# Rows 16 to 31 of the triangular matrices held in a PSUM bank for the substitution steps of a hybrid decoder trunk

## The chip, the cores and the metric

The kernel runs on one core of a Trainium2 chip. The metric is the device time of one execution in microseconds (us); lower is better. TensorE (PE in the profile) does the matrix products, VectorE (DVE), ScalarE (ACT) and GpSimd (POOL) the elementwise work, and SyncE (SP) issues the DMAs. Each engine works through a queue of instructions of its own.

## What is computed

Two layers of a decoder trunk on 512 tokens of width 1024. One input projection feeds three groups of heads side by side (RWKV-7 time mixing, causal pooling, native sparse attention); one output projection, a gated ConvFFN and a gated per-layer embedding follow. The change lies in the RWKV-7 mixer, whose recurrence over the tokens is

```
def step(S, inp):
    r_t, w_t, k_t, v_t, kk_t, a_t = inp
    sa = jnp.einsum('bhvk,bhk->bhv', S, -kk_t)
    S = (S * w_t[:, :, None, :] + sa[..., None] * (kk_t * a_t)[:, :, None, :]
         + v_t[..., None] * k_t[:, :, None, :])
    return S, jnp.einsum('bhvk,bhk->bhv', S, r_t)
...
_, y = lax.scan(step, S0, xs)
```

The kernel does it in chunks of 64 tokens. Within a chunk every token's `sa` depends on those of the tokens ahead of it in the chunk, which is a triangular system: for each of 8 chunks and 4 heads a 64x64 unit triangular matrix is inverted, 32 matrices in all for a layer.

## The kernel before

Everything is float32. A product that must be exact is split into a rounded part and its rest (`whi`, `wlo` for the weights, `xhl` for the activations) and done as three matmuls: L159, L160 and L161 in the helper `gemm`, 512 columns each. ACT makes `whi` (L132); `wlo` (L133) is made by POOL or by DVE, whichever a call of `wsplit` names.

The triangular matrices are inverted in 32x32 diagonal blocks. `IN` (tile `inn`, 128 partitions x 32 x 32) holds the blocks; the partitions are the 64 blocks (32 matrices, two blocks each), twice: DVE writes partitions 0 to 63 with a transpose (L415), ACT copies them to 64 to 127 (L417). The upper copy lets the lower half of the partitions work on even columns of the inverse and the upper half on odd ones. `QI` is the inverse, which POOL sets to the identity first (L421 to L423; `after(...)` makes the first of these wait for L417). Then the generator `rwkv()` runs 31 substitution steps on DVE, t = 1 to 31. Each is a multiply of the columns so far with row t of `IN`, broadcast over the columns (L434, m x (t+1) elements for each partition with m = (t+1)//2, into `prd`), and a sum of the products (L436, back into `QI`). After step 31 a copy (L438) and three transposes (L441 twice, L443) put the blocks where TensorE reads them. TensorE makes the off-diagonal blocks in two rounds of 32 small matmuls (L450 from `Q11`, shown as `q` in the trace, and then L458), and the recurrence over the eight chunks, `chain`, follows: per chunk the products g (L502, L506), u (L513), s (L521) and y (L536, L539).

Beside the substitution runs the projection work of the attention: `tokmaj` and `tokval` turn operands of the recurrence into token order on TensorE (L474 `bkt`, L485 `vt`), the projection onto tokens (L637 to L639, `tok`), the compression of keys and values (L654, `cmp`), and `roped` for four query tiles, then for two key tiles: a projection `z` of 24 matmuls, a shuffle of it (L588, DVE, from PSUM), a product with the cosines (L589, DVE, one operand in PSUM), two POOL instructions (L590, L591), a rounding on ACT (L599 or L596), the rest on DVE (L600 or L597), and DMAs into `qs` or `ku`. The compressed scores `sct` (L693) and their transposes `scp` (L707) stand on TensorE just ahead of L450. After L450 and L458 TensorE does two more projections (tiles p0 and p1 of `z`) between the first g, u and s, then the attention scores (L755 onwards).

What stands where on an engine is chosen ahead of time by a scheduler from the order in which the code is written, from `pace`, which slips pieces of `rwkv()` between the matmuls of `gemm`, and from the scheduler's own estimate of durations. The code hands out eight PSUM banks by tag: `rw` has three. `bkt`, `vt`, the blocks of L450 and L458, and all of `chain` take their banks from `rw`.

Of the kernel before, what the change touches and what calls it, by code (L numbers as in the profile page):

```python
# [12 lines left out]
ALU = mybir.AluOpType  # L13
AX = mybir.AxisListType

P = 128
# [27 lines left out]
def hybrid(tc, xT, pT, pos, cst, msk, par, gfin, w_in, w_tok, w_out, w_up, w_down, w_pg, w_pp,  # L44
           lora, wcmp, pe, wpool, out):
    nc = tc.nc
    V, S, G, TE = nc.vector, nc.scalar, nc.gpsimd, nc.tensor
    from contextlib import ExitStack
    ctx = ExitStack()
    with ctx:  # L50
# [8 lines left out]
        def nm(s):  # L59
            cnt[0] += 1  # L60
            return f"{s}_{cnt[0]}"
# [3 lines left out]
        def unit(shape, name, dt=F32, tag="r"):  # L65
            return mp.tile(shape, dt, tag=tag, name=nm(name), bufs=NB[tag])

        def psum(name, tag="sc"):
            return pp.tile([P, 512], F32, tag=tag, name=nm(name), bufs={"mm": 2, "rw": 3, "sc": 2, "o": 1}[tag])
# [189 lines left out]
        for l in range(L):  # L259
# [130 lines left out]
            for u in range(4):  # L390
                if u == 2:
                    mixed(7, VM[:, 1, :])
                for h2 in range(2):
                    a = slice(h2 * 64, h2 * 64 + 64)
# [19 lines left out]
            IN = unit([P, 32, 32], "inn")  # L414
            V.transpose(IN[0:64].rearrange("p a b -> p (a b)"), ND.rearrange("p a b -> p (a b)"))  # L415
            V.memset(IN[0:64].rearrange("p a b -> p (a b)")[:, 0:1024:33], 1.0)
            ti = S.copy(IN[64:128], IN[0:64])  # L417
            QI = unit([P, 32, 32], "qi")
            PRD = unit([P, 16, 32], "prd", tag="n")
            qf = QI.rearrange("p a b -> p (a b)")  # L420
# [9 lines left out]
            def rwkv():  # L430
                for t in range(1, 32):
                    m = (t + 1) // 2
                    qv = QI[:, 0:2 * m:2, :]
                    V.tensor_tensor(PRD[:, 0:m, 0:t + 1], qv[:, :, 0:t + 1],  # L434
                                    IN[:, t, 0:t + 1].unsqueeze(1).to_broadcast([P, m, t + 1]), op=ALU.mult)
                    V.tensor_reduce(qv[:, :, t], PRD[:, 0:m, 0:t + 1], axis=AX.X, op=ALU.add)  # L436
                    yield 0.3 + m * (t + 1) * 2.1e-3
                V.tensor_copy(QI[0:64, 1:32:2, :], QI[64:128, 0:32:2, :])  # L438
                Q11 = unit([32, 32, 32], "q11")
                for b in range(2):  # L440
                    V.transpose(TT_[b * 32:(b + 1) * 32, :, b * 32:(b + 1) * 32].rearrange("p i s -> p s i"),  # L441
                                QI[b * 32:(b + 1) * 32].rearrange("p j s -> p s j"))
                V.transpose(Q11.rearrange("p i j -> p j i"), QI[0:32])  # L443
                yield 4.0
                ZS = unit([64, 32, 32], "zs")
                for u in range(2):
                    ps = psum("z12", "rw")
                    for i in range(16):
                        n = u * 16 + i
                        TE.matmul(ps[32:64, i * 32:(i + 1) * 32], XM[n // 8][0:32, (n // 4) % 2, n % 4, 32:64],  # L450
                                  Q11[:, n, :], start=True, stop=True)
                    S.copy(ZS[32:64, u * 16:(u + 1) * 16, :].rearrange("p a b -> p (a b)"), ps[32:64, :])
                yield 1.5
                for u in range(2):
                    ps = psum("t12", "rw")
                    for i in range(16):
                        n = u * 16 + i
                        TE.matmul(ps[0:32, i * 32:(i + 1) * 32], ZS[32:64, n, :], TT_[32:64, n, 32:64],  # L458
                                  start=True, stop=True)
                    S.copy(TT_[0:32, u * 16:(u + 1) * 16, 32:64], ps[0:32, :].rearrange("p (a b) -> p a b", b=32))  # L460
                yield 1.5
                yp = None
                for c in range(NCK):
                    yp = yield from chain(c, yp)
# [27 lines left out]
            def chain(c, yp):  # L492
# [77 lines left out]
                return yp  # L570

            pace.start(rwkv(), 3.0)
            pace.tick(0.1)
            tokmaj()
# [66 lines left out]
            for t in range(4):  # L641
# [5 lines left out]
                            op=ALU.mult)  # L647
# [27 lines left out]
            for j in range(4):  # L675
# [4 lines left out]
                for g in range(2):  # L680
                    a = slice(g * 64, g * 64 + 64)
                    b = slice(64 - g * 64, 128 - g * 64)
# [19 lines left out]
            for cp2 in range(2):  # L702
# [6 lines left out]
                for c2 in range(2):  # L709
# [3 lines left out]
                                    op=ALU.add)  # L713
# [13 lines left out]
            for ty in range(2):  # L727
# [3 lines left out]
                for g in range(2):  # L731
                    a = slice(g * 64, g * 64 + 64)
                    b = slice(64 - g * 64, 128 - g * 64)
# [65 lines left out]
            for cp2 in range(2):  # L799
# [8 lines left out]
                for j2 in range(2):  # L808
                    a = slice(j2 * 64, j2 * 64 + 64)
# [148 lines left out]
            for n in range(KD):  # L958
# [5 lines left out]
                for h in range(HV):  # L964
                    a = slice(h * T // HV, (h + 1) * T // HV)
# [24 lines left out]
        for h in range(2):  # L990
            a = slice(h * 256, h * 256 + 256)
# [174 lines left out]
```

## Time and profile before

| | |
|---|---|
| median of three runs | 1508.69 us (1508.46 to 1509.61) |
| the profiled execution | 1512.75 us, of which the span from the first to the last instruction is 1511.0 us |
| TensorE busy | 1456.0 us, 96% of the span |
| VectorE, ScalarE, GpSimd busy | 824.3, 677.1 and 738.6 us |
| mean granted TensorE clock | 0.980 of full speed |

The profile is of one execution. Its page gives the busy time of each engine; the timeline lists instructions in order with the idle time ahead of each and what ended it; the windows give busy time and granted clock of chosen stretches. A TensorE matmul's shown duration overlaps the next one's, so the pace is read from one start to the next. [...]

### The profile page before, as it was taken

The page shows a single profiled execution, that of the slowest core. Times are in us where ns is not written, and L with a number is a line of the kernel's source. Part 1 is how long each engine was busy: PE and PEld are TensorE (multiplying, and loading weights), DVE is VectorE, ACT ScalarE, POOL GpSimd, SP SyncE. Part 2 cuts the span into 40 slices and gives each one's busy share as a digit, 9 for nine tenths or more (in the row PEclk, how much of TensorE's full clock was granted, in tenths as well). Part 3 has the DMA queues.
Part 4 walks back from the last instruction along what each step waited for, and adds up shares of the span by engine and source line. Part 5 has one row for each costly group of instructions (what it writes and reads, how often), then busy time and mean ns, then how long its engine had stood idle before and what let it go on. Part 6 is the DMA issues. An engine that isn't in the chain of part 4 may idle for free.

```text
span 1511.0 us, 21122 instructions
## 1 busy us (share of the span) xinstructions
PE 1456.0 (96%) x7634; PEld 1161.9 (77%) x7634; DVE 824.3 (55%) x1354; ACT 677.1 (45%) x1296; POOL 738.6 (49%) x621
## 2 busy tenths in 40 slices
PE   6999899999999999999999989899999999999997
PEld 4787666588888888888877867666888888888886
DVE  7769687425773155522567696772277712554234
ACT  5552265544443245443544425564454423444433
POOL 3355443275455455566614553533645555555653
PEclk9999799999999999999999989999999999999998
DMA  5234400042233333333422243001422333333332
GB/s 174 67 98 116 107 3 2 19 144 86 97 98 100 103 97 95 97 99 103 150 90 75 82 118 84 2 15 56 126 91 94 98 96 103 96 100 93 97 100 95
DMA packets 78985, 134.62 MB, mean 89 GB/s; under 512 B 10145, under 2 KB 20897, under 8 KB 78881
## 3 DMA queue, kind: packets, MB, share of 16 engines
q1 hardware_dynamic: 77728, 132.22, 29.2%
q8 instruction: 60, 0.98, 0.3%
q10 hardware_dynamic: 1152, 1.05, 0.2%
q14 instruction: 45, 0.36, 0.1%
HBM read 120.59 MB, written 4.19 MB: 83 GB/s over the span
## 4 chain that ended last, share of the span: by engine, by line
PE 84%; DVE 12%; issue 2%; ACT 1%; POOL 0%; DMA 0%; SPq 0%; DVEq 0%; ACTq 0%
PE up L161 11%; PE up L159 11%; PE up L160 11%; PE dn L161 5%; PE dn L159 5%; PE dn L160 5%; PE o L864 2%; PE z L161 2%; PE z L159 2%; PE ptp L856 2%; PE z L160 2%; PE wo L159 2%; PE wo L160 2%; PE wo L161 2%; PE pg L160 2%; PE pg L159 2%
## 5 line engine op out<-in xcount | busy, mean ns | idle before, releaser
L133 POOL TENSOR_TENSOR wlo<-raw,whi 128x512 fp32r<-128x512 f32 (+3 forms) x392 | 507.8, 1299 | 476.7 <-ACT whi L132 463.7
L132 ACT CAST whi<-raw 128x512 fp32r<-128x512 f32 (+3 forms) x440 | 261.2, 596 | 433.7 <-PE up L160 114.4
L159 PE MATMUL up<-xhl,whi 128*128 128x512 f32 x704 | 274.1, 389 | 0.0
L161 PE MATMUL up<-xhl,wlo 128*128 128x512 f32 x704 | 273.7, 389 | 0.0
L160 PE MATMUL up<-xhl,whi 128*128 128x512 f32 x704 | 273.6, 389 | 0.0
L160 PEld LDWEIGHTS up<-xhl,whi 128*128 128x128 f32 x704 | 132.1, 188 | 27.5
L161 PEld LDWEIGHTS up<-xhl,wlo 128*128 128x128 f32 x704 | 132.1, 188 | 27.5
L159 PEld LDWEIGHTS up<-xhl,whi 128*128 128x128 f32 x704 | 132.1, 188 | 27.2
L159 PE MATMUL dn<-ghl,whi 128*128 128x512 f32 x352 | 136.9, 389 | 0.0
L160 PE MATMUL dn<-ghl,whi 128*128 128x512 f32 x352 | 136.9, 389 | 0.0
L161 PE MATMUL dn<-ghl,wlo 128*128 128x512 f32 x352 | 136.3, 389 | 0.0
L159 PE MATMUL z<-xhl,whi 128*128 128x512 f32 x288 | 117.8, 410 | 7.3 <-ACT whi L132 6.4
L929 DVE SCALAR_TENSOR_TENSOR cv<-cv,par 128x511 f32<-128x511 f32 x88 | 77.9, 885 | 82.2 <-ACT cv L928 82.2
L161 PE MATMUL z<-xhl,wlo 128*128 128x512 f32 x288 | 116.6, 405 | 4.6 <-DVE wlo L133 4.6
L160 PE MATMUL z<-xhl,whi 128*128 128x512 f32 x288 | 116.5, 405 | 4.0 <-DVE xhl L192 3.9
L944 DVE TENSOR_TENSOR x<-x,dn 128x512 f32<-128x512 f32 x32 | 22.0, 688 | 166.4 <-PE dn L161 166.4
L931 DVE SCALAR_TENSOR_TENSOR cv<-cv,par 128x510 f32<-128x510 f32 x88 | 100.3, 1142 | 2.9
L927 DVE TENSOR_TENSOR cv<-up,rb 128x512 f32<-128x512 f32 x88 | 60.0, 684 | 74.1 <-PE up L161 59.8
L771 ACT ACTIVATE pb<-sc,smax 128x128 f32<-128x128 f32 (+3 forms) x128 | 66.8, 531 | 46.5 <-DVE smax L768 26.0
L928 ACT ACTIVATE cv<-cv,par 128x512 f32<-128x512 f32 x88 | 71.6, 815 | 31.4 <-DVE cv L927 31.4
L160 PEld LDWEIGHTS dn<-ghl,whi 128*128 128x128 f32 x352 | 66.1, 188 | 13.8
L161 PEld LDWEIGHTS dn<-ghl,wlo 128*128 128x128 f32 x352 | 66.1, 188 | 13.7
(299 smaller groups left out, 2626.2 us busy)
## 6 DMA issues: line engine op xcount, KB each, us to landing
raw<-in_w_up_dram SPq DMA_DIRECT2D x176, 256.0 KB, 2.7
raw<-in_w_in_dram SPq DMA_DIRECT2D x72, 256.0 KB, 2.8
raw<-in_w_down_dram SPq DMA_DIRECT2D x64, 256.0 KB, 2.6
raw<-in_w_out_dram SPq DMA_DIRECT2D x32, 256.0 KB, 2.8
raw<-in_w_pg_dram SPq DMA_DIRECT2D x32, 256.0 KB, 2.7
raw<-in_w_down_dram SPq DMA_DIRECT2D x32, 192.0 KB, 2.3
x<-in_xT_dram SPq DMA_DIRECT2D x16, 256.0 KB, 3.8
qs<-hl SPq DMA_DIRECT2D x32, 128.0 KB, 2.3
```

Source lines behind the costliest of these rows:

```text
L132: S.copy(hi[:, :ncol], raw[:, :ncol])
L133: (lo_eng or G).tensor_tensor(lo[:, :ncol], raw[:, :ncol], hi[:, :ncol].bitcast(F32), op=ALU.subtract)
L159: TE.matmul(ps, wh, xh, start=i == 0, stop=False)
L160: TE.matmul(ps, wh, xl, start=False, stop=False)
L161: TE.matmul(ps, wl, xh, start=False, stop=i == n - 1)
L771: S.activation(pb[:, ty, 0:w], srcs[ty], AF.Exp, bias=smax[:, g, ty:ty + 1], accum_out=ssum[:, g, ty:ty + 1])
L856: TE.transpose(ps[:, (g * 2 + j2) * P:(g * 2 + j2 + 1) * P], pbs[j2][g][:, ty, kb * P:(kb + 1) * P], ident)
L864: TE.matmul(op_[g * 64:g * 64 + 64, 0:256], VT[:, kb, ty * 128 + g * 64:ty * 128 + g * 64 + 64], pts[ty][:, g, :], start=False, stop=kb == ...
L927: V.tensor_tensor(u_, ps, rb, op=ALU.mult)
L928: S.activation(c_, u_, AF.Identity, scale=pc(PC2 + n), bias=pc(PCB + n))
L929: V.scalar_tensor_tensor(c_[:, 1:T], u_[:, 0:T - 1], pc(PC1 + n), c_[:, 1:T], op0=ALU.mult, op1=ALU.add)
L931: V.scalar_tensor_tensor(c_[:, 2:T], u_[:, 0:T - 2], pc(PC0 + n), c_[:, 2:T], op0=ALU.mult, op1=ALU.add)
```

## The change

Only rows 0 to 15 of `IN`, columns 0 to 15, are copied by ACT into partitions 64 to 127 now. A new tile `INP` takes one of the three `rw` banks; ACT copies rows 16 to 31 of `IN` into both of its halves, from partitions 0 to 63 (two copies of 64 x 512). Steps t = 16 to 31 read row t from `INP`, steps 1 to 15 from `IN` as before. `INP` holds its bank until step 31 has read it. Arithmetic and its order within a step are unchanged. Lines from 422 on stand four lines lower in the new kernel.

```diff
-            ti = S.copy(IN[64:128], IN[0:64])
+            ti = S.copy(IN[64:128, 0:16, 0:16], IN[0:64, 0:16, 0:16])
+
+            INP = psum("inp", "rw").rearrange("p (a b) -> p a b", b=32)
+            for b in range(2):
+                S.copy(INP[b * 64:(b + 1) * 64], IN[0:64, 16:32, :])
...
                     V.tensor_tensor(PRD[:, 0:m, 0:t + 1], qv[:, :, 0:t + 1],
-                                    IN[:, t, 0:t + 1].unsqueeze(1).to_broadcast([P, m, t + 1]), op=ALU.mult)
+                                    (IN[:, t, 0:t + 1] if t < 16 else INP[:, t - 16, 0:t + 1]).unsqueeze(1).to_broadcast([P, m, t + 1]), op=ALU.mult)
```

The scheduler gives a new order from here on. On VectorE, around step 15 of the first layer, it was (`ct`, `kcm` and `vcin` are small steps of the compressed keys that wait for `cmp` of TensorE; `wlo` is a weight's rest; `zt` and `qr` are the shuffle and the product of the first query tile):

```order
L133 TENSOR_TENSOR wlo_1293<-raw_1290,whi_1292 128x512
L434 TENSOR_TENSOR prd_681<-qi_680,inn_676 128x8x17
L436 TENSOR_REDUCE qi_680<-prd_681 128x8
L434 TENSOR_TENSOR prd_681<-qi_680,inn_676 128x9x18
L436 TENSOR_REDUCE qi_680<-prd_681 128x9
L588 STREAM_SHUFFLE zt_1269<-z_1146 128x512
L434 TENSOR_TENSOR prd_681<-qi_680,inn_676 128x9x19
```

and is now

```order
L438 TENSOR_TENSOR prd_684<-qi_683,inn_676 128x8x16
L661 COPY ct_1135<-cmp_1102 128x2x33
L440 TENSOR_REDUCE qi_683<-prd_684 128x8
L663 TENSOR_TENSOR kcm_1137<-ct_1135 128x64
L438 TENSOR_TENSOR prd_684<-qi_683,inp_680 128x8x17
L671 COPY vcin_1143<-kcm_1137 128x128
```

The `wlo` step that stood ahead of step 16 has moved ahead of step 11, and the small steps of the compressed keys have moved from steps 11 to 13 to steps 15 and 16. On TensorE, ahead of `cmp`, all of `tok` now comes before the first `bkt`, 14 matmuls of the first query tile stand ahead of `cmp` (2 before), and one group of four `vt` has moved from ahead of the end of `cmp` to behind it.

On TensorE, around the two rounds of small matmuls of the first layer, it was (`sct` and `scp` are the compressed scores and their transposes, `z_239`, `z_240` the first round, `t_241`, `t_242` the second, `g` the first product of the recurrence)

```order
L693 MATMUL sct_1612<-qs_1600,KC_1136 32x512 x2
L693 MATMUL sct_1612<-qs_1489,KC_1136 32x512 x2
L707 MATMUL scp_1618<-cst,sct_1605 128x128 x4
L707 MATMUL scp_1635<-cst,sct_1605 128x128 x4
L450 MATMUL z_239_1163<-q_216_1048,xm_568 32x32 x8
L450 MATMUL z_239_1163<-q_216_1048,xm_569 32x32 x8
L450 MATMUL z_240_1181<-q_216_1048,xm_570 32x32 x8
L450 MATMUL z_240_1181<-q_216_1048,xm_571 32x32 x8
L458 MATMUL t_241_1208<-Tinv,zs_1162 32x32 x16
L458 MATMUL t_242_1226<-Tinv,zs_1162 32x32 x16
L502 MATMUL g_1250<-uv_685,xm_568 64x64 x4
```

and is now

```order
L697 MATMUL sct_1615<-qs_1492,KC_1139 32x512 x2
L711 MATMUL scp_1621<-cst,sct_1608 128x128
L454 MATMUL z_240_1166<-q_217_1051,xm_568 32x32 x8
L454 MATMUL z_240_1166<-q_217_1051,xm_569 32x32 x8
L454 MATMUL z_241_1184<-q_217_1051,xm_570 32x32 x8
L454 MATMUL z_241_1184<-q_217_1051,xm_571 32x32 x8
L711 MATMUL scp_1621<-cst,sct_1608 128x128 x3
L711 MATMUL scp_1638<-cst,sct_1608 128x128 x4
L462 MATMUL t_242_1211<-Tinv,zs_1165 32x32 x16
L462 MATMUL t_243_1229<-Tinv,zs_1165 32x32 x16
L506 MATMUL g_1253<-uv_688,xm_568 64x64 x4
```

Seven of the eight transposes `scp` have moved behind the first round of small matmuls.

In the second layer the attention's stage before stood in another order than in the first. On TensorE, at the end of the projection p0 and p1 (`z`) and the first scores (`sc`), it was

```order
L159 MATMUL z_8479<-xhl_6528,whi_8488 128x512
L160 MATMUL z_8479<-xhl_6528,whi_8488 128x512
L755 MATMUL sc_8343<-ku_8135,qs_7760 128x256
L755 MATMUL sc_8366<-ku_8135,qs_7848 128x256
L161 MATMUL z_8479<-xhl_6528,wlo_8489 128x512
L521 MATMUL s_7785<-uv_7184,bkt_7186 64x64 x4
L539 MATMUL y_7798<-uv_7184,xm_7067 64x64 x4
L502 MATMUL g_7806<-uv_7184,xm_7067 64x64 x4
```

and is now

```order
L159 MATMUL z_8485<-xhl_6655,whi_8494 128x512
L160 MATMUL z_8485<-xhl_6655,whi_8494 128x512
L161 MATMUL z_8485<-xhl_6655,wlo_8495 128x512
L525 MATMUL s_7791<-uv_7190,bkt_7192 64x64 x4
L543 MATMUL y_7804<-uv_7190,xm_7070 64x64 x4
L506 MATMUL g_7812<-uv_7190,xm_7070 64x64 x4
L759 MATMUL sc_8349<-ku_8141,qs_7766 128x256
L760 MATMUL sc_8349<-ku_8142,qs_7766 128x256
```

With the change both layers have one and the same order on every engine through this stage, and from the first scores on, save a handful of neighbours that have changed places, it is the order that the first layer had before.

## Rows read from the trace of the kernel before

**Rows 1.** The page's first part: for each engine busy time, share of the span and instructions.

```profile
PE 1456.0 (96%) x7634; PEld 1161.9 (77%) x7634; DVE 824.3 (55%) x1354; ACT 677.1 (45%) x1296; POOL 738.6 (49%) x621
```

**Rows 2.** The waits of TensorE: who waited for whom, us in total, times, longest.

```profile
PE z L450 <- DVE q L443: 6.0, 2, 3.7
...
PE sct L693 <- issue: 2.5, 1, 2.5
```

**Rows 3.** Windows of the first layer through the substitution: length, then busy time (and instructions) of PE, PEld (weight loads), DVE, ACT and POOL, granted clock, DMA share and rate.

```profile
100.00:120.00 20.00, 20.00 (x172) 17.79 (x171) 11.75 (x44) 10.43 (x23) 7.94 (x10) 1.00 0.28 83
120.00:150.00 30.00, 29.24 (x130) 22.25 (x129) 29.19 (x47) 9.01 (x15) 18.48 (x13) 1.00 0.50 133
150.00:160.00 10.00, 4.12 (x20) 2.05 (x18) 9.84 (x10) 1.20 (x2) 4.36 (x3) 0.73 0.40 127
```

**Rows 4.** Windows at the half clock in both layers: from the first small matmul to the first product of p0, and on to the return of the full clock.

```profile
160.72:168.54 7.82, 7.82 (x137) 7.64 (x137) 5.62 (x11) 2.67 (x5) 3.79 (x3) 0.50 0.01 2
168.54:171.68 3.14, 3.14 (x8) 2.49 (x8) 2.57 (x7) 1.21 (x3) 0.00 (x0) 0.50 0.55 121
899.91:907.73 7.82, 7.82 (x136) 7.64 (x137) 7.14 (x13) 3.71 (x7) 3.79 (x3) 0.50 0.06 14
907.73:912.20 4.47, 4.47 (x12) 3.51 (x12) 3.62 (x10) 0.68 (x2) 0.00 (x0) 0.50 0.89 199
```

**Rows 5.** VectorE's timeline of the first layer, the steps 18, 22, 23 and 29 (L434): start, duration, engine, line, operation, out<-in, size.

```profile
121.17 1.36 DVE L434 TENSOR_TENSOR prd<-qi,inn 128x171 f32<-128x171 f32 x1
...
127.25 0.42 DVE L434 TENSOR_TENSOR prd<-qi,inn 128x253 f32<-128x253 f32 x1
...
130.79 1.54 DVE L434 TENSOR_TENSOR prd<-qi,inn 128x288 f32<-128x288 f32 x1
...
145.88 1.11 DVE L434 TENSOR_TENSOR prd<-qi,inn 128x450 f32<-128x450 f32 x1
```

**Rows 6.** GpSimd's timeline at the same times, with the idle time ahead and what ended it in brackets.

```profile
121.03 1.30 POOL L133 TENSOR_TENSOR wlo<-raw,whi 128x512 fp32r<-128x512 f32 x1 [6.27 <-ACT whi L132]
...
129.02 1.29 POOL L590 TENSOR_TENSOR zt<-zt,rt 128x512 f32<-128x512 f32 x1 [2.51 <-DVE zt L588]
130.40 1.62 POOL L591 TENSOR_TENSOR qr<-qr,zt 128x512 f32<-128x512 f32 x1
...
143.28 1.53 POOL L590 TENSOR_TENSOR zt<-zt,rt 128x512 f32<-128x512 f32 x1 [2.36 <-DVE zt L588]
144.89 1.62 POOL L591 TENSOR_TENSOR qr<-qr,zt 128x512 f32<-128x512 f32 x1
```

**Rows 7.** VectorE's timeline: instructions of 512 and of 128 elements with one operand in PSUM (L589, L670) and with both in SBUF (L133, L600, L434).

```profile
116.02 0.29 DVE L434 TENSOR_TENSOR prd<-qi,inn 128x128 f32<-128x128 f32 x1
...
122.44 0.28 DVE L670 TENSOR_TENSOR VC<-vct,cst 128x128 f32<-128x128 f32 x1
...
134.81 0.68 DVE L600 SCALAR_TENSOR_TENSOR hl<-qr,hl 128x512 fp32r<-128x512 f32 x1
...
143.58 0.69 DVE L589 TENSOR_TENSOR qr<-z,rt 128x512 f32<-128x512 f32 x1
144.18 1.18 DVE L133 TENSOR_TENSOR wlo<-raw,whi 128x512 fp32r<-128x512 f32 x1
```

**Rows 8.** Windows of the first layer from step 16 to the end of step 31, with VectorE's instructions of one line alone, their busy time and count: first L434, then L436, then L133 (its first is the tail of one that began ahead of the window).

```profile
118.84:152.93 34.09, 15.73 (x16) 1.00 0.51 138
...
118.84:153.66 34.82, 7.46 (x16) 1.00 0.50 136
...
118.84:152.93 34.09, 3.75 (x5) 1.00 0.51 138
```

**Rows 9.** ScalarE's timeline of the first layer: the copy of `IN`, and copies of 64 x 512 elements between PSUM and SBUF.

```profile
101.60 1.05 ACT L417 COPY inn<-inn 64x1024 f32<-64x1024 f32 x1
...
113.79 0.58 ACT L489 COPY uv<-vt 64x512 f32<-64x512 f32 x1 [3.91 <-PE vt L485]
```

**Rows 10.** VectorE's timeline of the first layer, a wait in the early steps, the start of step 16, and the transposes after step 31.

```profile
114.03 0.23 DVE L657 COPY ct<-cmp 128x66 f32<-128x66 f32 x1 [3.07 <-PE cmp L654]
...
118.85 0.30 DVE L434 TENSOR_TENSOR prd<-qi,inn 128x136 f32<-128x136 f32 x1
...
158.76 1.90 DVE L443 STREAM_TRANSPOSE q<-qi 32x1024 f32<-32x1024 f32 x1
```

**Rows 11.** TensorE's timeline of the first layer: two of the last projection's matmuls, the compressed scores and transposes, the small matmuls, and the projections after them, with the change of pace.

```profile
150.08 0.39 PE L160 MATMUL z<-xhl,whi 128*128 128x512 f32 x1
150.31 0.39 PE L161 MATMUL z<-xhl,wlo 128*128 128x512 f32 x1
153.23 1.32 PE L693 MATMUL sct<-qs,KC 128*32 128x512 f32 x8 [2.53 <-issue]
...
155.28 1.75 PE L707 MATMUL scp<-cst,sct 128*128 128x128 f32 x7 [0.37 <-ACT sct L700]
160.72 3.46 PE L450 MATMUL z<-q,xm 32*32 32x32 f32 x61 [3.69 <-DVE q L443]
...
168.54 0.80 PE L159 MATMUL z<-xhl,whi 128*128 128x512 f32 x1
```

**Rows 12.** TensorE's timeline where the output projection begins, in the first and in the second layer.

```profile
294.20 0.50 PE L159 MATMUL wo<-yh,whi 128*128 128x512 f32 x1
...
1035.54 0.50 PE L159 MATMUL wo<-yh,whi 128*128 128x512 f32 x1
```

## Prediction

> **What bounds the kernel now.** I read the page first: TensorE is busy 96% of the span [rows 1], so a change on VectorE, busy 55%, can only pay where TensorE waits for it or runs slow because of it. Then TensorE's waits: among the longest is the one of the small matmuls L450 for the transpose L443 that ends the substitution, 6.0 us in two layers, 3.7 in the first; the compressed scores wait 2.5 us just ahead of it [rows 2]. The windows show the stage: from 120 to 150 us both engines are full (TensorE 29.24, VectorE 29.19 of 30), from 150 to 160 VectorE stays full (9.84 of 10) and TensorE is busy for 4.12 only, and its granted clock falls from 1.00 to a mean of 0.73 [rows 3]. [...] So here, and in the second layer, VectorE's substitution sets the end, and TensorE pays twice: in idle time and in clock.
>
> Next, what VectorE does in that stretch. Step 18 multiplies 171 elements in 1.36 us, step 22 needs 0.42 us for 253 [rows 5]. Beside GpSimd's timeline the pattern is plain: step 18 begins at 121.17 while GpSimd is in L133 from 121.03 to 122.33, and ends 0.2 us after that; step 22 falls into a gap of GpSimd (idle until 129.02); step 23 ends 0.31 us after the L591 that ran to 132.02, step 29 0.48 us after the one that ran to 146.51 [rows 5, 6]. The step waits for GpSimd's instruction to end and then does its own elements. An instruction with one operand in PSUM does not: L589 takes 0.69 us for 512 elements in the midst of GpSimd's L590, and the L133 right behind it, with both operands in SBUF, takes 1.18 us and ends 0.55 us after that same L590 [rows 6, 7].
>
> **The change part by part.** (1) The waits of the multiplies. The 16 steps from t = 16 take 15.73 us in L434 and 7.46 us in L436, which reads the same number of elements with one operand; step 22 and the 0.42 us show that an undisturbed multiply costs what its sum costs. So 15.73 - 7.46 = 8.3 us per layer are waits [rows 5, 8], and with `INP` as the second operand they go. The bounds: 0, if a PSUM operand of this form waits as well, and 8.3; L589 is the nearest row and speaks for 8.3. Does a PSUM operand cost more by itself? The pairs say no: 0.69 us against 0.68 at 512 elements, 0.28 against 0.29 at 128 [rows 7]; I take 0. [...]
>
> (2) The early steps. ScalarE's copy shrinks from 64 x 1024 to 64 x 256 elements (1.05 us; by the 0.58 us of 512 elements [rows 9] about 0.35), and two copies of 0.58 us are added: 0.5 us more on ScalarE, ahead of the first weights of the query projection. TensorE has the rest of `tok` in front of it there and is busy for all of 100 to 120 us [rows 3], so I cost it at nothing; uncovered it would be 0.5. VectorE's start: it waits for `cmp` until 114.03 with 3.07 us idle, and step 16 begins at 118.85 [rows 10]. Now `cmp` ends behind 12 more projection matmuls (12 x 0.23 = 2.8 us by the pace of [rows 11]) and ahead of four `vt` (0.4 us by my estimate), so about 116.4; but steps 11 to 15 are then already done, and the `wlo` that held step 16 back is too. Step 16 should begin near 116.9: 1.9 us earlier. Bounds 0 and 2.
>
> (3) What takes the place of the waits. In the stretch four L133 and four L600 on VectorE also have both operands in SBUF. They waited little so far, 3.75 - 0.09 (tail) - 4 x 0.68 = 0.94 us for L133 [rows 7, 8] and nothing for the L600 that the rows show (0.68), because the multiply ahead of them had sat out GpSimd's instruction. Now they will meet it: GpSimd is busy 18.48 of 30 us [rows 3], a wait is on average half an instruction, 0.7 us, so 8 x 0.62 x 0.7 = 3.5, or 2.5 more than now. Bounds 0 and 6.
>
> Sum on VectorE: 8.3 + 1.9 - 2.5 = 7.7 us, so L443 ends near 153.0 instead of 160.66 [rows 10]. Is TensorE there by then? Its last projection ended at 150.54 with 0.76 us of waits behind it from 120 us on [rows 3, 11]; without them 149.8, then `sct` 1.1, ScalarE's copy 0.6, one `scp` 0.25: 151.8. VectorE still decides, by about 1.2 us, and the 2.53 us wait ahead of `sct` should be gone, since the last query tile's L600 comes several us earlier. L450 begins 7.7 us earlier.
>
> (4) The clock. In the trace it fell after TensorE had stood still for 2.53 us, then done 3 us of light work and stood again for 3.69 [rows 11]. What is left is idle for 0.6 and 1.2 us. I take it that the clock stays. Then the 7.82 us at 0.50 from L450 to the first product of p0 [rows 4] become 3.9, plus the seven `scp` that now stand in between (1.75 us at the half clock [rows 11], 0.9 at the full), plus 0.4 for copies: 5.2, 2.6 less. The 8 projection matmuls that followed in 3.14 us take 1.8: 1.3 less. In the second layer 12 matmuls in 4.47 us become 2.8: 1.7 less [rows 4].
>
> (5) The second layer's order. From L450 to the output projection it took 1035.54 - 899.91 = 135.6 us against 294.20 - 160.72 = 133.5 in the first [rows 4, 11, 12], and it now has the first layer's order. Of the 2.1 us, 0.4 are in (4) already; how much of 1.7 is order and how much chance can't be told; I take half, 0.9.
>
> First layer 7.7 + 2.6 + 1.3 = 11.6, second 7.7 + 2.6 + 1.7 = 12.0, order 0.9: 24.5 us. What follows is a chain through TensorE, so I let the shift go through to the end. Against the profiled execution of 1512.75 us that is 1488.2; the median of the runs lies 4.06 below the profiled one, so 1508.69 - 24.5 = 1484.2.
>
> **The rivals.** *The clock falls all the same*, over the pauses that are left around the small matmuls. Then L450 to p0 costs 7.82 + 1.75 = 9.6 us at the half clock, and p0 begins at 162.6 instead of 168.54: 5.9 per layer, with 0.9 12.7 us, 1496.0. For it: the idle pieces are shorter, not gone. If it falls in one layer only, 24.5 - 5.9 = 18.6, 1490.
>
> *The waits pass on.* L133, L600 and what depends on them take 6 us of the 8.3, and the clock falls: VectorE gains 8.3 + 1.9 - 6 = 4.2, of which the exposed 1.75 us of `scp` takes back part: 2.4 per layer and 0.9, 5.8 us, 1502.9. For it: L133's 1.18 us [rows 7]; against it: eight instructions only.
>
> *The operand in PSUM doesn't help*, and the step waits as before. Then 1.9 - 1.75 per layer is left and 0.9: 1507.5, no change that can be told.
>
> *The bank is missed.* `INP` holds one of three `rw` banks until step 31, and `bkt` and `vt` (eight fills) turn over the two that are left, each waiting for ScalarE's copy. TensorE would stand at three turnovers, with `cmp` and every projection behind it in the queue, and VectorE behind these. A copy can be as late as the 3.91 us for which one waited in this trace [rows 9]: 3 x 3.9 = 11.7 a layer. With the clock down as well, which such pauses would bring about, that is 11.7 - 5.9 = 5.8 slower a layer, 1508.7 + 11.6 - 0.9 = 1519. It decides from 6 us a layer on. Against it: projection and `cmp` matmuls stand between the pairs.
>
> **How the numbers follow.** Forecast with the clock up 0.42; down in one layer 0.20; down in both 0.20; waits passed on 0.10; no help 0.04; bank 0.04. The likeliest gives 1484.2; its own range, by the bounds of (2), (3) and (5), is 1479 to 1490. For 8 in 10 the range takes in the clock's cases: 1479 to 1499. About 0.2%, 3 us, can be told from no change: faster 0.92, same 0.04, slower 0.04.
>
> **What would show it.** L434 from t = 16 near 7.5 us a layer, with L133 and L600 longer than now; step 16 near 116.9; L450 near 153 us with about 1 us of wait; the clock at 1.00 from 150 to 175; p0 near 158; `wo` of the first layer near 282.6. Wrong it would be if multiplies above t = 15 still end with GpSimd's instructions, if TensorE waits at `bkt` or `vt`, or if the 0.50 stretch is still there.

## The result and the profile after

| | before | after |
|---|---|---|
| median, us | 1508.69 (1508.18 to 1514.03, five runs) | 1500.49 (1498.54 to 1502.03, five runs) |
| the profiled execution, its span | 1512.75, 1511.0 | 1498.75, 1497.0 |
| mean granted TensorE clock | 0.980 | 0.987 |

The ratio is 0.9935, 95% interval 0.9923 to 0.9947: faster by 8.2 us, where 24.5 were forecast, and 1.5 us outside the range. Of all runs told of here one, of the changed kernel in e1, was a slow one (1805.74 us at a granted clock of 0.747) and enters no median.

What was meant to go has gone. Windows of the changed kernel from step 16 to the end of step 31, VectorE's instructions of one line alone, first the multiplies (L438, which was L434), then their sums (L440), then L133; they answer to [rows 8]:

```profile
117.17:145.60 28.43, 7.50 (x16) 1.00 0.49 130
...
117.17:146.30 29.13, 7.46 (x16) 1.00 0.51 132
...
117.17:146.30 29.13, 3.90 (x4) 1.00 0.51 132
```

The sixteen multiplies now cost what their sums cost, 7.50 us for 15.73. VectorE's timeline of the changed kernel, answering to [rows 5, 7, 10], with step 16 first, step 22 (253 elements), an L133, step 31 and the transpose for which TensorE waits:

```profile
117.17 0.29 DVE L438 TENSOR_TENSOR prd<-qi,inp 128x136 f32<-128x136 f32 x1
...
123.13 0.29 DVE L674 TENSOR_TENSOR VC<-vct,cst 128x128 f32<-128x128 f32 x1 [1.98 <-PE vct L672]
...
125.42 0.42 DVE L438 TENSOR_TENSOR prd<-qi,inp 128x253 f32<-128x253 f32 x1
...
130.44 1.23 DVE L133 TENSOR_TENSOR wlo<-raw,whi 128x512 fp32r<-128x512 f32 x1
...
144.39 0.68 DVE L438 TENSOR_TENSOR prd<-qi,inp 128x512 f32<-128x512 f32 x1
...
151.63 1.90 DVE L447 STREAM_TRANSPOSE q<-qi 32x1024 f32<-32x1024 f32 x1
```

GpSimd's timeline beside it, answering to [rows 6]:

```profile
124.98 1.30 POOL L133 TENSOR_TENSOR wlo<-raw,whi 128x512 fp32r<-128x512 f32 x1 [0.61 <-ACT whi L132]
...
129.51 1.62 POOL L595 TENSOR_TENSOR qr<-qr,zt 128x512 f32<-128x512 f32 x1
```

Step 22, with its operand in PSUM, runs from 125.42 to 125.84 inside GpSimd's L133 and takes the same 0.42 us that it took in a gap of GpSimd before. The L133 of VectorE, both operands in SBUF, still ends 0.54 us after GpSimd's L595. So the mechanism is seen in both halves: the operand in PSUM freed the instruction from the wait, two operands in SBUF did not. A new line is the `VC` step that waits 1.98 us for TensorE. The transpose L447 ends at 153.53 (160.66 before).

Now what did not come. TensorE's waits, answering to [rows 2]:

```profile
PE z L454 <- DVE q L447: 4.3, 2, 2.1
```

TensorE's timeline of the first layer, answering to [rows 11]:

```profile
151.13 0.33 PE L711 MATMUL scp<-cst,sct 128*128 128x128 f32 x1
153.59 2.21 PE L454 MATMUL z<-q,xm 32*32 32x32 f32 x64 [2.13 <-DVE q L447]
155.72 1.23 PE L711 MATMUL scp<-cst,sct 128*128 128x128 f32 x7
156.88 3.62 PE L462 MATMUL t<-Tinv,zs 32*32 32x32 f32 x64
...
161.47 0.80 PE L159 MATMUL z<-xhl,whi 128*128 128x512 f32 x1
162.07 0.63 PE L160 MATMUL z<-xhl,whi 128*128 128x512 f32 x1
```

and windows, answering to [rows 3] and [rows 4]: the stretch up to the wait, then from the first small matmul to p0 and on to the return of the pace of 0.23 us, in both layers:

```profile
120.00:150.00 30.00, 30.00 (x142) 23.56 (x141) 27.33 (x51) 9.79 (x16) 20.61 (x16) 1.00 0.56 149
...
153.59:161.47 7.88, 7.88 (x143) 7.33 (x143) 4.56 (x9) 2.67 (x5) 2.53 (x2) 0.67 0.05 16
161.47:166.34 4.87, 4.87 (x13) 3.81 (x13) 3.77 (x9) 1.32 (x3) 1.53 (x1) 0.50 0.51 113
886.45:896.08 9.63, 9.63 (x143) 9.06 (x144) 4.63 (x9) 2.67 (x5) 2.53 (x2) 0.52 0.04 13
896.08:900.60 4.52, 4.52 (x12) 3.60 (x12) 3.77 (x9) 1.32 (x3) 1.52 (x1) 0.52 0.48 107
```

TensorE is now full from 120 to 150 us, and its waits ahead of `sct` are gone, as forecast; but it still stands for 2.1 us ahead of the small matmuls in each layer, and the granted clock still falls, to 0.50: in the first layer the 64 matmuls of L454 (the trace shows two for each of the 32 of the program) still take 2.21 us, the full pace, and those of L462 3.62, the half pace; in the second layer nearly all of the stretch is slow.

### The profile page after: what moved, and what is told of

Its sections match the earlier page's. It is cut to its first block, busy times and chain, and to the rows that moved or that the text cites. A ratio compares the mean times of both kernels' runs of the same rounds, so it can differ in the third digit from the quotient of the medians.

```text
span 1497.0 us, 21104 instructions
## 1 busy us (share of the span) xinstructions
PE 1451.1 (97%) x7634; PEld 1159.6 (77%) x7634; DVE 816.1 (55%) x1354; ACT 677.0 (45%) x1300; POOL 733.6 (49%) x621
## 4 chain that ended last, share of the span: by engine, by line
PE 84%; DVE 10%; ACT 2%; issue 1%; POOL 1%; DMA 0%; DVEq 0%; SPq 0%; ACTq 0%; POOLq 0%
PE up L161 11%; PE up L159 11%; PE up L160 11%; PE dn L159 5%; PE dn L160 5%; PE dn L161 5%; PE z L161 3%; PE z L159 3%; PE z L160 3%; PE o L868 2%; PE ptp L860 2%; PE wo L159 2%; PE wo L160 2%; PE wo L161 2%; PE pg L159 2%; PE pg L160 2%
## 5 line engine op out<-in xcount | busy, mean ns | idle before, releaser
L133 POOL TENSOR_TENSOR wlo<-raw,whi 128x512 fp32r<-128x512 f32 (+3 forms) x392 | 503.2, 1287 | 474.9 <-ACT whi L132 441.7
```

The source lines that it names most:

```text
L133: (lo_eng or G).tensor_tensor(lo[:, :ncol], raw[:, :ncol], hi[:, :ncol].bitcast(F32), op=ALU.subtract)
```

## The experiments

| label | edit | median, us | ratio to before, interval | waits for the Q11 transpose, us | z12 to p0, us (layer 1, 2) |
|---|---|---|---|---|---|
| e1_again | none (changed kernel) | 1500.18 | 0.9931 [0.9919, 0.9943] | 4.3 | 9.09, 9.15 |
| e2_sbuf_read | bank filled, but not read | 1511.38 | 1.0004 [0.9995, 1.0012] | 7.0 | 7.82, 7.82 |
| e3_q11_first | Q11's transpose first | 1489.11 | 0.9853 [0.9837, 0.9870] | none | 7.36, 6.40 |
| e4_fill | 8 wide matmuls in the wait | 1493.54 | 0.9892 [0.9879, 0.9906] | none | 6.87, 5.80 |
| e5_before_again | none (kernel before) | 1508.39, one run | | 5.0 | 7.82, 7.82 |
| e6_q11_before | kernel before, Q11's transpose first | 1506.82 | 0.9975 [0.9966, 0.9984] | 0.3 | 9.82, 9.82 |
| e7_q11_fill | e3 and 8 wide matmuls among the small | 1489.79 | 0.9865 [0.9850, 0.9880] | none | 7.90, 7.89 |
| e8_small_fill | the wide matmuls among the small, wait kept | 1500.7 | 0.9944 [0.9929, 0.9960] | 4.2 | 10.83, 10.86 |

The kernel before ran beside each group, with medians of 1510.82 (e1 to e4), 1510.48 (e5 to e7) and 1509.46 (e8). "z12" is the first small matmul (L450, later L454), "p0" the first projection matmul behind them; the columns are differences of start times in each profile.

**e1_again.** The changed kernel once more, without an edit.

> The changed kernel once more, unchanged, for a second profile and more runs. If the 14.0 us between the two profiled executions (1512.75 and 1498.75) were the gain and the 8.2 us between the medians a chance of the runs, the median should come out near 1495. If the profiled execution of the kernel before was a long one of its kind, the median stays at 1498 to 1502, 7 to 10 us under the kernel before, and the new profile's stages differ from the first one's by microseconds in stages that the change doesn't touch.

Median and ratio come out again, the wait too, and the fall. Windows of this run, first layer and second:

```profile
155.00:160.00 5.00, 5.00 (x81) 4.61 (x78) 1.73 (x6) 1.15 (x2) 1.26 (x1) 0.57 0.01 5
160.00:165.00 5.00, 5.00 (x61) 4.62 (x60) 3.72 (x7) 2.40 (x5) 1.26 (x1) 0.50 0.02 6
890.00:895.00 5.00, 5.00 (x71) 4.61 (x69) 2.57 (x6) 0.95 (x2) 0.82 (x2) 0.50 0.00 0
```

**e2_sbuf_read.** The bank is taken and filled, but every step reads its row in SBUF.

```diff
-            ti = S.copy(IN[64:128, 0:16, 0:16], IN[0:64, 0:16, 0:16])
+            ti = S.copy(IN[64:128], IN[0:64])
...
-                                    (IN[:, t, 0:t + 1] if t < 16 else INP[:, t - 16, 0:t + 1]).unsqueeze(1).to_broadcast([P, m, t + 1]), op=ALU.mult)
+                                    IN[:, t, 0:t + 1].unsqueeze(1).to_broadcast([P, m, t + 1]), op=ALU.mult)
```

> The bank is held and filled as in the change, but all 31 steps read IN in SBUF, copied in full to the upper partitions. Theory, that the gain comes from where the operand of steps 16 to 31 lies: the 16 multiplies take about 15.7 us a layer again, with the ends of GpSimd's instructions as their ends, and the time is that of the kernel before or up to 4 us more (two more copies on ScalarE, one bank fewer): 1508 to 1513. Rival, that the gain comes from the new order of the early steps (the weight's rest moved ahead of step 11, step 16 about 1.7 us earlier): it keeps 3 us or more of the gain, under 1506, if that order stays.

The whole gain is gone, ratio 1.0004, so it doesn't come from the copies or the bank. Whether it comes from the new order this run doesn't tell by its time: behind `cmp` the scheduler here went back to the order of before, with the `scp` ahead of z12, and of the new order it kept that of the early steps alone. What speaks for the operand is the multiplies' own time: the sixteen take 15.68 us again. The windows of these multiplies, and VectorE's timeline of this run, the steps 29, 30 and 31:

```profile
120.70:155.10 34.40, 15.68 (x16) 1.00 0.49 131
...
147.69 1.11 DVE L438 TENSOR_TENSOR prd<-qi,inn 128x450 f32<-128x450 f32 x1
...
150.45 1.73 DVE L438 TENSOR_TENSOR prd<-qi,inn 128x465 f32<-128x465 f32 x1
...
153.38 1.33 DVE L438 TENSOR_TENSOR prd<-qi,inn 128x512 f32<-128x512 f32 x1
```

Step 29 takes 1.11 us again, as in [rows 5], and step 31 1.33 for 0.68 with the PSUM operand. Holding the bank costs nothing that shows (ratio 1.0004).

**e3_q11_first.** TensorE waits for the last of three transposes, of which its first small matmuls need only that one. Here it goes first.

```diff
+                V.transpose(Q11.rearrange("p i j -> p j i"), QI[0:32])
                 for b in range(2):
                     V.transpose(TT_[b * 32:(b + 1) * 32, :, b * 32:(b + 1) * 32].rearrange("p i s -> p s i"),
                                 QI[b * 32:(b + 1) * 32].rearrange("p j s -> p s j"))
-                V.transpose(Q11.rearrange("p i j -> p j i"), QI[0:32])
```

> The changed kernel with the transpose that the first round of small matmuls waits for put ahead of the two that only the second round needs. Theory, that the forecast missed because TensorE still waits about 2.1 us for that transpose and its clock falls over this wait: the wait goes, the transpose is ready at about 149 us and TensorE comes at 151.5; if the clock stays at 1.00 from 150 to 175 us, p0 begins near 156.5 instead of 161.47 and its first matmuls run at the full pace, 6 us a layer, so 12 us less than the changed kernel, about 1488. If the clock falls all the same, over the small matmuls themselves, only the 2.1 us go, about 4 in all, 1496. Rival, that what was won is given back after p0 (order, banks): p0 earlier, but the output projection not earlier than in the changed kernel by more than 1 us a layer, 1499.

1489.11 us, 11.1 under the changed kernel of e1, for one line moved; TensorE's order is the same in both. The wait is gone and the time is near the theory's 1488, though the theory had the clock up throughout and it is not. Windows of this run in the first layer:

```profile
150.00:155.00 5.00, 5.00 (x84) 3.51 (x82) 4.92 (x5) 2.37 (x4) 1.35 (x2) 1.00 0.34 108
155.00:160.00 5.00, 5.00 (x75) 4.63 (x74) 4.25 (x10) 2.09 (x4) 2.45 (x2) 0.55 0.01 4
160.00:165.00 5.00, 5.00 (x18) 4.02 (x17) 3.48 (x9) 1.88 (x4) 2.18 (x2) 0.76 0.63 140
```

TensorE is busy in all of these 15 us and waits for nobody, and the clock falls nonetheless, after 64 matmuls of 32x32 and seven `scp`, and in the midst of 64 more. In the second layer it falls too, later (z12 to p0 takes 6.40 us). It comes back earlier: the half pace of the projection ends at 162.2 us, in the changed kernel at 166.3.

**e4_fill.** The order of the transposes stays, and the wait is filled with eight matmuls whose result nothing uses.

```diff
+                du = psum("du", "rw")
+                for i in range(8):
+                    mi = TE.matmul(du, identR, xs[i][0], start=True, stop=True)
+                    if i == 0:
+                        after(mi, tt)
                 V.transpose(Q11.rearrange("p i j -> p j i"), QI[0:32])
```

> The changed kernel with eight matmuls of 512 columns whose result is not used, held back until the second of the three transposes, so that TensorE works on them in the 2.1 us in which it waited for the third. They take 1.8 us at the full pace. Theory (the clock falls over the wait): the clock stays at 1.00 and p0 begins near 158.4 instead of 161.47, 4 us a layer with its first matmuls at the full pace, 1492. Rival (it falls over the small matmuls, whatever is ahead of them): the clock falls after 153 us as before, p0 comes at 161 to 162, the time is that of the changed kernel, 1500 to 1502. Third, the stage after p0 decides: no gain with the clock at 1.00.

6.6 us under the changed kernel of e1, although the small matmuls start no earlier (44.27 us after `cmp`, 44.13 in the changed kernel): the gain lies behind them, where the clock is the difference. In the second layer it stayed up, in the first it fell after all. Windows of this run, two of each layer:

```profile
155.00:160.00 5.00, 5.00 (x124) 4.79 (x122) 2.85 (x8) 1.73 (x3) 1.66 (x2) 0.89 0.03 9
160.00:165.00 5.00, 5.00 (x28) 4.15 (x27) 4.71 (x9) 2.26 (x4) 2.33 (x2) 0.50 0.24 52
...
885.00:890.00 5.00, 5.00 (x101) 4.23 (x100) 2.85 (x7) 1.15 (x2) 1.26 (x1) 1.00 0.17 52
890.00:895.00 5.00, 5.00 (x67) 4.37 (x64) 5.00 (x10) 3.10 (x6) 1.64 (x2) 1.00 0.18 41
```

So the wait was one cause and not the only one. The second layer also gives the stretch's price at the full clock: z12 to p0 in 5.80 us.

**e5_before_again.** A second profile of the kernel before, to see what of the first was chance.

> The kernel before, unchanged, profiled a second time. The prediction's sum was made against a profiled execution of 1512.75 us, 4.1 us above the median of 1508.69, in which the second layer's attention stretch (scores to wo) took 105.51 us against 99.79 in the first layer. Theory: that execution was a long one, and part of its excess lies in that stretch of the second layer, since another kernel with the same order there took 102.23. Then this profile is shorter: scores to wo of the second layer 100 to 104 us, span 1507 to 1510; the first layer's stretches (compress to z12 51.7, 99.8 from scores to wo) come out again within 0.6 us. Rival: the stretch is a fixed price of the order of the kernel before; then it takes 105 to 106 again and the span is 1510 to 1512.

The span is 1506.6 us, 4.4 shorter. Windows of the second layer, 960 to 980 us, of the first profile of before and then of this one:

```profile
960.00:980.00 20.00, 17.30 (x128) 12.68 (x128) 13.07 (x31) 8.00 (x22) 8.36 (x11) 0.83 0.00 1
```

```profile
960.00:980.00 20.00, 17.31 (x160) 12.55 (x158) 16.10 (x40) 11.05 (x30) 8.81 (x13) 1.00 0.00 1
```

The execution that the prediction was worked out from had one more fall of the clock there. From p0 to the up projection the second layer took 171.47 us in it, 167.23 in this one and 167.35 in e2, which has the same order. The first layer's stretches come out again (51.71 us from `cmp` to z12, 7.82 to p0). Scores to `wo` took 102.51 us, as the theory of chance has it; the span lies 0.4 us under its range and far from the rival's.

**e6_q11_before.** The same line moved in the kernel before; nothing in PSUM.

> The kernel before with one line moved: the transpose that makes Q11, for which TensorE waits, stands ahead of the two transposes into TT_; no row of the triangular matrices is in PSUM. In the run with both, this order took 11.4 us off the changed kernel (1500.5 to 1489.1), 4.2 of them TensorE's waits. Theory: what the order gives is the 2.2 us per layer by which z12 starts earlier, and, on the changed kernel, most of a fall of the clock, since there the wait goes to nothing. Here z12 waits 7.0 us in both layers together (3.69 and 3.3), so about 1.5 per layer is left, TensorE still stops ahead of z12 and the clock falls as before; the time is 4.4 us under before, 1504 to 1507, ratio 0.995 to 0.998. Rival: the order alone carries most of the 11.4 us, whatever the operands are; then 1497 to 1500, ratio 0.991 to 0.994, and the PSUM copy and the order are worth about the same.

1506.82 us: the time expected by the theory, 3.7 under before, but by other steps than it says. TensorE's timeline of this run:

```profile
155.47 2.05 PE L693 MATMUL sct<-qs,KC 128*32 128x512 f32 x8 [2.93 <-issue]
157.46 0.48 PE L707 MATMUL scp<-cst,sct 128*128 128x128 f32 x1
158.20 3.62 PE L450 MATMUL z<-q,xm 32*32 32x32 f32 x64 [0.26 <-DVE q L440]
161.75 1.75 PE L707 MATMUL scp<-cst,sct 128*128 128x128 f32 x7
163.43 3.62 PE L458 MATMUL t<-Tinv,zs 32*32 32x32 f32 x64
```

The wait for Q11 shrinks to 0.26 us, not to 1.5, and z12 comes 47.34 us after `cmp`, 4.4 earlier than in e5. But the multiplies still wait for GpSimd, TensorE stands for 2.93 us ahead of `sct`, and everything from there on runs at the half clock (`sct` 2.05 us, 1.06 in e7 at the full); seven `scp` now lie in the stretch, at 1.75 us. The transpose first gives 0.25% by itself, the change by itself 0.69 (e1), both 1.47 (e3), more than their sum: only with both does TensorE not stand at all in this stretch.

**e7_q11_fill.** e3 with four wide matmuls behind each round of small ones, their results unused.

```diff
                     S.copy(ZS[32:64, u * 16:(u + 1) * 16, :].rearrange("p a b -> p (a b)"), ps[32:64, :])
+                du = psum("du", "rw")
+                for i in range(4):
+                    TE.matmul(du, identR, xs[i][0], start=True, stop=True)
...
                     S.copy(TT_[0:32, u * 16:(u + 1) * 16, 32:64], ps[0:32, :].rearrange("p (a b) -> p a b", b=32))
+                du = psum("du", "rw")
+                for i in range(4, 8):
+                    TE.matmul(du, identR, xs[i][0], start=True, stop=True)
```

> The changed kernel with Q11's transpose first, and beside it in each layer 8 matmuls of 128x512 whose results nothing uses: 4 behind the z12 matmuls and 4 behind the t12 matmuls, that is in the stretch of 32x32 matmuls in which TensorE never waits but the granted clock still fell (155 to 160 us at 0.55, 160 to 165 at 0.76 with Q11 first). They cost 8 x 0.23 = 1.8 us per layer where the clock holds. Theory: after the wait is gone it is the small matmuls themselves that let the clock fall, and wide ones between them hold it: 150 to 170 us at 1.00, the p0 matmuls at 0.39 us from the first on (0.63 in six of them before), p0 begins 1.8 less 0.5 later per layer, and the time is within 2 us of 1489.1. Rival: the fall has nothing to do with what TensorE does in that stretch; then the clock stands at 0.5 to 0.6 somewhere in 155 to 165 again, the matmuls only add their time, and it is 1492 to 1494.

The clock holds, in both layers. Windows of this run, two of each:

```profile
155.00:160.00 5.00, 5.00 (x86) 4.16 (x84) 4.23 (x9) 1.91 (x4) 2.47 (x2) 1.00 0.01 4
160.00:165.00 5.00, 5.00 (x23) 4.15 (x23) 4.35 (x9) 2.16 (x4) 3.16 (x2) 1.00 0.60 133
...
885.00:890.00 5.00, 5.00 (x71) 4.17 (x69) 5.00 (x10) 2.94 (x5) 1.76 (x2) 1.00 0.13 29
890.00:895.00 5.00, 5.00 (x27) 3.92 (x26) 4.36 (x10) 1.76 (x3) 3.09 (x3) 1.00 0.79 176
```

The time is e3's within their intervals: what the clock gives, the unused matmuls take. So without a wait it is the small matmuls by themselves, as the theory said, after which the clock falls (0.55 over 155 to 160 us in e3, 1.00 here).

**e8_small_fill.** The wide matmuls of e7 in the changed kernel, whose wait stays.

> The changed kernel with its own order of the transposes, so that TensorE still waits some 2.1 us ahead of z12 in each layer, and with the 8 unused matmuls of 128x512 in the stretch of small matmuls (4 behind z12, 4 behind t12). It is the fourth corner of a square: wait and no wide matmuls (the changed kernel) fell to 0.50 in both layers, no wait and none fell for a shorter time, no wait and wide ones held 1.00 throughout. Theory A: the wait alone is enough for a fall; then the clock stands at 0.50 somewhere in 153 to 165 us of the first layer, wide matmuls or not, and the time is 1500.5 plus up to 3.6, 1500 to 1504. Theory B: the narrow matmuls decide and a wait of 2.1 us by itself does nothing; then 1.00 throughout, z12 to p0 takes 7.9 us, p0 to the scores 13.3, and the time is that of the run with both plus the 4.4 us that z12 starts later, 1493 to 1496.

Theory A held in full, on clock and time. TensorE's timeline of this run:

```profile
154.94 3.19 PE L454 MATMUL z<-q,xm 32*32 32x32 f32 x64 [2.14 <-DVE q L447]
158.07 2.08 PE L459 MATMUL du<-xhl,cstr 128*128 128x512 f32 x4
159.94 1.70 PE L717 MATMUL scp<-cst,sct 128*128 128x128 f32 x7
161.57 2.54 PE L465 MATMUL t<-Tinv,zs 32*32 32x32 f32 x64
164.04 1.19 PE L470 MATMUL du<-xhl,cstr 128*128 128x512 f32 x4
```

Windows of the same run:

```profile
154.90:155.50 0.60, 0.56 (x17) 0.56 (x18) 0.60 (x1) 0.00 (x0) 0.00 (x0) 1.00 0.60 208
155.70:162.30 6.60, 6.60 (x71) 5.71 (x70) 1.38 (x4) 1.15 (x2) 1.22 (x1) 0.50 0.00 0
```

The clock falls within L454, less than 1 us after the wait and ahead of the first wide matmul, and is back within L465 (the last four wide matmuls take 1.19 us, the first four 2.08), where the changed kernel stayed at 0.50 into the projection. So in this stretch the wait of 2.1 us was enough for a fall, with wide matmuls to follow, and the small matmuls were enough without a wait: in both layers of e3, and in one of the two of e4, where wide matmuls stood right ahead of them. With neither there was none (e7).

## Why the prediction was wrong

To compare stretch by stretch, e5 stands for the kernel before (span 1506.6) and the changed kernel's first profile for after (1497.0), 9.6 us apart:

| stretch | before (layer 1, 2) | after (layer 1, 2) | gain | forecast |
|---|---|---|---|---|
| `cmp` to z12, steps (1) to (3) | 51.71, 51.72 | 44.13, 44.14 | 15.2 | 15.4 |
| z12 to p0, first part of (4) | 7.82, 7.82 | 7.88, 9.63 | -1.9 | 5.2 |
| p0 to the up projection, rest of (4) and (5) | 170.05, 167.23 | 170.30, 169.94 | -3.0 | 3.9 |
| all else | | | -0.7 | 0 |

**Step (1) was right:** 15.73 - 7.50 = 8.2 us for 8.3. The operand in PSUM cost these instructions nothing by itself that shows: sixteen of them took 7.50 us beside 7.46 for their sums.

**Step (2) was right:** step 16 at 117.17 for 116.9, and `cmp` was there for VectorE at 116.71 for 116.4. The 0.4 us for four `vt` was the author's estimate, which no run shows: such a group takes 1.09 us in the traces of both kernels.

**Step (3) was right in its sum and not in its parts.** From step 16 to the end of step 31 the stretch shortened by 34.82 - 29.13 = 5.7 us, with 8.2 less in the multiplies: 2.5 us were taken, as forecast. But VectorE's L133 and L604 wait hardly longer than before (3.90 - 4 x 0.68 = 1.18 us against 0.94, and 2.84 in L604 against 2.72), so 0.4 us in place of 2.5. What took the rest is another wait, which the prediction did not see: VectorE comes to `VC` at 121.15, earlier than before ([rows 7]: 122.44, without a wait), and stands for 1.98 us, since TensorE has two groups of `vt`, eight matmuls each in the trace, from 120.0 to 122.5 us ahead of `vct`. That the sum came out is luck. TensorE was ready at 151.46, a little ahead of the 151.8 forecast, and VectorE half a microsecond behind its 153.0; so the wait was 2.13 and not 1.2.

**Step (4) failed**, in the sentence "I take it that the clock stays". It rests on a misreading of [rows 11], that the clock fell only after two waits. Windows of the kernel before, two of each layer, ahead of the fall and behind it:

```profile
150.00:154.60 4.60, 2.07 (x13) 0.67 (x11) 4.46 (x8) 0.62 (x1) 3.50 (x3) 1.00 0.52 162
154.70:160.70 6.00, 1.96 (x8) 1.35 (x7) 5.97 (x5) 0.52 (x1) 0.76 (x1) 0.50 0.27 87
...
889.90:891.80 1.90, 0.00 (x0) 0.00 (x0) 1.87 (x3) 0.29 (x1) 1.55 (x2) 1.00 0.87 264
892.00:893.00 1.00, 0.00 (x0) 0.00 (x0) 0.93 (x3) 0.62 (x1) 1.00 (x1) 0.50 0.60 199
```

In the first layer the clock fell some 1.4 us after the wait of 2.53 us ahead of `sct`, with the wait of 3.69 still to come; in the second it fell inside the wait of 3.21 us ahead of `sct`, behind wide matmuls alone. So one such wait had been enough. The change removed these two, but the wait ahead of the small matmuls was only shortened, from 3.69 us to 2.13 in the first layer and from 2.33 to 2.14 in the second, and the clock fell. e8 shows that such a wait is enough here, and e3 that even without it the small matmuls would have brought a fall. Of the 5.2 us between z12 and p0, 1.9 were lost instead, since the seven `scp` now stand in that stretch at the half clock: the second layer's 9.63 us are the 9.6 that the rival "the clock falls all the same" worked out. At the full clock the stretch takes 5.80 (e4), so even then step (4) was 0.6 a layer too large.

**Step (5) had the wrong sign.** What it takes for the beginning of the output projection, 294.20 and 1035.54 us ([rows 12]), are later matmuls of it; its first stand at 283.01 and 1025.64. The 2.1 us are right even so if taken up to the up projection (177.15 and 179.29 us from z12 in that execution). The second layer of before seemed slow by 2.1 us because of the extra fall in that one execution. In e5 and e2 its old order took 167.23 and 167.35 us from p0 to the up projection, at the half clock at its start; the new order takes 169.94 and, in e1, 168.94, and even with the clock up throughout 168.00 (e7). The old order of that layer was the better one, even so by some 0.7 us.

**The rival** had the mechanism, and 12.7 us; the table has 9.6: 1.5 more up to p0, where the first layer fell only in part, 3.9 less behind it, the wrong sign of (5) above all, and 0.7 less elsewhere. The medians lie around that, 8.2 us in the first five runs and 10.6 in e1. The other rivals fell: the multiplies' time shows that the operand in PSUM helps (7.50 us, and 15.68 in e2 with the operand in SBUF), and e2 that holding the bank costs nothing that shows (ratio 1.0004).

**Open:** why in e4 the clock stayed up in one layer and fell in the other, with the same order of work, and in which executions an extra fall comes (the changed kernel has such falls too: in e1 the clock is at 0.50 from 80.7 to 83.9 and from 814.5 to 817.7 us). No run holds the new order fixed and moves only the operand, so what the order alone is worth up to z12 is not shown.

## What to carry over

A wait that is shortened and not removed can keep its price in the clock (2.1 us of wait were left here, and the clock fell to 0.50): of the 15.2 us by which the small matmuls came earlier in two layers, 9.6 were left at the end. When the transpose that TensorE needed was also put first, that one moved line brought 11.1 us, about as much as the change itself. Read from the windows where the clock falls before you say which wait brought it down. Ask of a stretch of tiny matmuls what the granted clock does in it even if TensorE is busy throughout (0.55 over 155 to 160 us in e3), and put wide work that has to be done anyway among them (tried here only with unused matmuls, which pay back just what they cost, 1489.79 us for 1489.11). Take a second profile of the kernel before, before a difference between two of its layers is called an effect of order.

## What the hardware showed that was not expected

- TensorE at 100% busy in the windows, with no wait, went from 1.00 to a mean of 0.55 over 155 to 160 us (e3); eight matmuls of 128x512 put between, and it stayed at 1.00 (e7).
- That the operand in PSUM frees the multiply from waiting for GpSimd was forecast; that it does so to the hundredth was not: step 22 took 0.42 us in the midst of GpSimd's L133, and 0.42 in a gap before.
- Where nothing disturbs the clock, executions repeat almost exactly: from the first `up` matmul to the first `pg`, at 1.00 in the windows of both kernels, both layers took 362.24 or 362.25 us in the profiles of the kernel before, the changed kernel, e3, e4, e7 and e8. Differences of a microsecond can be read off a single profile there, and can't around a fall of the clock (z12 to p0 in the changed kernel: 7.88 and 9.09 us in two executions).
